# Attention scores of a hybrid trunk: keys stored once, two heads on the two row halves of the array

## The chip, the core and the metric

The kernel runs on one core of a Trainium2 chip. A core has TensorE (PE, the matrix unit; its weight loads are shown as PEld), VectorE (DVE), ScalarE (ACT), GpSimd (POOL) and SyncE (SP), which issues most of the DMAs. Each engine takes its own instructions in the order in which they stand, and waits on semaphores for the others. The metric is the device time of one execution in microseconds, lower is better; the figure compared is the median of several runs.

## The reference

A two-layer decoder trunk for 256 tokens with 1024 features, all in float32. Layer 0 mixes tokens by native sparse attention (NSA), layer 1 by RWKV-7; each is followed by a squared-ReLU MLP. The change touches NSA alone. It has 16 heads of width 64 in 4 groups; the 4 heads of a group share keys and values. Three branches are added with learned gates: compressed keys, selected blocks and a window. With 256 tokens all causal blocks are selected and the window covers everything, so these two branches see the same causal mask and differ in their keys and values:

```
s_s = einsum(q, k_selected) * scale ; p_s = softmax(where(valid_s, s_s, -1e30))
s_w = einsum(q, k_window)   * scale ; p_w = softmax(where(valid_w, s_w, -1e30))
o   = g0 * (p_c @ v_compressed) + g1 * (p_s @ v_selected) + g2 * (p_w @ v_window)
x   = x + concat(o) @ w_out
```

## The kernel before

Weights are streamed from HBM in 512 KB chunks and split into two float32r parts (ACT makes the high one on line 229, DVE the low one on line 231), and every product with weights is the sum of three matmuls (lines 265 to 267). The layer's work is written out once, as a list of steps in `NSA_ORDER`; a scheduler that simulates a timeline then fixes the order of the instructions of PE, ACT, DVE and POOL, and which of the free PSUM slots a tile gets. Only SP's queue stands as written. PSUM is one pool with two tags of four slots, each slot one 2 KB bank: `pmm` for tiles that PE fills and others read soon, `pacc` for accumulators.

The steps that matter here: `T0` and `T1` run `keys()` and `queries()`, which transpose keys and queries on PE. `qT[gp]` holds two heads of a pair one above the other: head s=0 in partitions 0 to 63, head s=1 in 64 to 127. The two heads belong to the two groups of a group pair. `kT[gp]` holds the keys of both groups, once for each s, with the other group's 64 partitions set to zero by a memset on POOL, so that a matmul over all 128 rows gives the scores of one head.

Steps `s0` to `s7` run `scores(pr)` for the eight pairs of heads. For a head, query tile t=0 sees 128 keys and t=1 sees 256, in both branches: one matmul 128x256 (S0, line 623) and one 128x512 (S1, line 625). The two S0 of a pair share one PSUM tile; each S1 has its own. On line 630 DVE adds the mask, takes the maximum, and writes the masked scores `e` to SBUF, once for a branch; ACT then makes the exponentials (line 634). `weigh` scales `e` (DVE, line 649), transposes it on PE (lines 652 to 654, tiles p) and copies the result out (lines 656, ACT and 659, DVE). `values` accumulates the output `po` of a pair: first the compressed branch, whose probabilities `pcT` come from `compressed(gp)` (transposes pcp on line 708, copy on DVE on line 709), as a matmul of 32 rows (line 665), then the two other branches with one head in each column half of the array (lines 670 and 673). Lines 674 and 675 take `po` out. Around these steps PE has the projection of the second half of the queries (acc), and after them the product with `w_out`, for which all `po` are wanted.

The RWKV layer is not touched by the change. Four of its names come up: for a chunk of tokens PE makes pZ (lines 1170, 1172), ACT copies it to Zt (line 1173), PE makes pQ from Zt (line 1179), and ACT copies pQ to VS (line 1180). ACT also squares the layer's output (ysq, line 1223), which belongs to the normalisation of an earlier chunk.

Of the kernel before, what the change touches and what calls it, by code (L numbers as in the profile page):

```python
# [9 lines left out]
F32 = mybir.dt.float32  # L10
# [23 lines left out]
# per-feature vectors, [128, 8] columns each  # L34
# [5 lines left out]
LAG = 2           # feed-forward tiles between the two products of the MLP  # L40
TAIL = 4          # weight chunks at the end of a product that are used by one token tile after the other
NF = DFF // 128
NPERM, NMID, NSLOT = 12, 18, 29       # 4 KB slots: for all layers, from the first feed-forward layer on, with RWKV's


def _mlp_order():
    """(product, feed-forward tile) in the order of use."""
    o, done = [], 0
    for f in range(NF):
        o.append((0, f))  # L50
        if f >= LAG and done < NF - TAIL:
            o.append((1, done))
            done += 1
    return o + [(1, f) for f in range(done, NF)]


# ---------------------------------------------------------------- host layout
def _consts():
    """Arrays that depend on shapes alone, side by side in one [128, n] block."""
# [20 lines left out]
    # cumulative sums about the middle of a chunk: columns t = -1 .. C-1  # L80
# [91 lines left out]
# ---------------------------------------------------------------- the kernel  # L172
@with_exitstack
def trunk(ctx: ExitStack, tc: tile.TileContext, wb, x_in, wg, cw1k, cw1v, cw2, vecs_in, l1, w2, a2, g2, rows,
# [44 lines left out]
    # ---- weights: streamed in 1 MB chunks, cut into two float32r parts  # L219
# [18 lines left out]
    # 4 KB slots, handed out in program order  # L238
# [24 lines left out]
    def mm3(o, lh, ll, rh, rl, first, last):  # L263
        """o += (lh + ll).T @ (rh + rl), without the product of the two low parts."""
# [20 lines left out]
    def after_split():  # L285
        """What this block traces on ACT and DVE comes after the last split of a layer's input."""
# [6 lines left out]
    def transposed_split(src, gv, h, l, t, name, cbs=(0, 1)):  # L293
        """h + l = (src * g).T, columns of token tile t."""
# [15 lines left out]
    def gemm_parts(hT, lT, evac, ncols, ahead=None):  # L310
        """Token-major product with the next weight chunks, 512 columns at a time."""
# [15 lines left out]
    def out_proj(hT, lT, name, after, tail=TAIL, hold=(), own=2):  # L327
        """x += (hT + lT).T @ the next weight chunks, then after(t): one token tile at a time, from the last chunks on."""
# [29 lines left out]
        for t in range(NT):  # L358
            # the second tile's first half of the columns ends before its second one
# [71 lines left out]
    # ================================================================ NSA  # L431
    def nsa():
        with ExitStack() as es:
            pool = es.enter_context(tc.tile_pool(name="nsa", bufs=1))
            kc = [big([128, 2 * G, 2, DH], f"kc{t}") for t in range(NT)]   # every head twice
# [897 lines left out]
```

## Time and profile before

| | us |
|---|---|
| runs shown | 761.9, 762.09, 764.71 (median 762.09) |
| span of the profiled execution | 758.7 |
| PE busy, share | 742.6, 98% |
| DVE busy, share | 468.5, 62% |
| ACT busy, share | 422.7, 56% |
| PE share of the chain that ended last | 96% |

The span reaches from the first to the last instruction of one profiled execution; the time of that execution itself is not given, and the span lies 3.4 us under the median of the runs. The scores, from the first S to the last `po`, stand between 69 and 140 us. A matmul in float32 is written as two records, its two passes through the array, and matmuls overlap in the records, so the time that one takes is better read from start to start than from its duration. "x2" in a row of the timeline counts records.

### The profile page before, as it was taken

The page shows a single profiled execution, that of the slowest core. Times are in us where ns is not written, and L with a number is a line of the kernel's source. Part 1 is how long each engine was busy: PE and PEld are TensorE (multiplying, and loading weights), DVE is VectorE, ACT ScalarE, POOL GpSimd, SP SyncE. Part 2 cuts the span into 40 slices and gives each one's busy share as a digit, 9 for nine tenths or more (in the row PEclk, how much of TensorE's full clock was granted, in tenths as well). Part 3 has the DMA queues.
Part 4 walks back from the last instruction along what each step waited for, and adds up shares of the span by engine and source line. Part 5 has one row for each costly group of instructions (what it writes and reads, how often), then busy time and mean ns, then how long its engine had stood idle before and what let it go on. Part 6 is the DMA issues. An engine that isn't in the chain of part 4 may idle for free.

```text
span 758.7 us, 13485 instructions
## 1 busy us (share of the span) xinstructions
PE 742.6 (98%) x5286; PEld 634.4 (84%) x5286; DVE 468.5 (62%) x963; ACT 422.7 (56%) x870; POOL 61.1 (8%) x77
## 2 busy tenths in 40 slices
PE   7999999999999999999999999999999999999996
PEld 5876866789989989888898885798989889989995
DVE  5767798358454455567856698546667444544553
ACT  6627587247555555563656642444729465565562
POOL 1000000000000000001012610136110000000000
PEclk9999999999999999999999999699999999999999
DMA  8956200218565555680152261320315655555531
GB/s 285 333 172 223 86 27 11 78 53 320 188 191 192 176 190 194 206 280 16 42 181 68 85 189 34 108 98 17 113 55 176 212 187 182 188 185 181 189 112 55
DMA packets 32013, 111.51 MB, mean 147 GB/s; under 512 B 3629, under 2 KB 4141, under 8 KB 31950
## 3 DMA queue, kind: packets, MB, share of 16 engines
q1 hardware_dynamic: 30590, 107.89, 42.7%
q10 hardware_dynamic: 1216, 2.24, 1.1%
q8 instruction: 41, 0.67, 0.4%
q0 software_dynamic: 144, 0.52, 0.2%
q14 instruction: 22, 0.18, 0.1%
HBM read 108.54 MB, written 1.05 MB: 144 GB/s over the span
## 4 chain that ended last, share of the span: by engine, by line
PE 96%; DVE 1%; issue 1%; DMA 1%; ACT 1%; SPq 0%; POOLq 0%; POOL 0%; ACTq 0%; DVEq 0%
PE mu L266 8%; PE mu L265 8%; PE mu L267 8%; PE mo L267 8%; PE mo L265 8%; PE mo L266 8%; PE acc L266 3%; PE acc L265 3%; PE acc L267 3%; PE pa L266 2%; PE pa L265 2%; PE pa L267 2%; PE S L625 2%; PE pM L1037 2%; PE po L670 1%; PE pL L975 1%
## 5 line engine op out<-in xcount | busy, mean ns | idle before, releaser
L231 DVE TENSOR_TENSOR wl<-wst,wh 128x1024 fp32r<-128x1024 f32 x175 | 214.3, 1229 | 177.2 <-ACT wh L229 176.4
L229 ACT ACTIVATE wh<-wst 128x1024 fp32r<-128x1024 f32 x175 | 184.4, 1058 | 166.7 <-PE mu L266 77.5
L266 PE MATMUL mo<-wl,mqh 128*128 128x512 f32 x224 | 88.4, 395 | 0.0
L265 PE MATMUL mo<-wh,mqh 128*128 128x512 f32 x224 | 88.2, 395 | 0.0
L267 PE MATMUL mo<-wh,mql 128*128 128x512 f32 x224 | 87.5, 397 | 0.0
L266 PE MATMUL mu<-m1l,wh 128*128 128x256 f32 x256 | 72.4, 284 | 0.0
L265 PE MATMUL mu<-m0h,wh 128*128 128x256 f32 x256 | 71.5, 281 | 0.4 <-DVE m0l L303 0.4
L267 PE MATMUL mu<-m1h,wl 128*128 128x256 f32 x256 | 71.8, 281 | 0.0
L265 PE MATMUL mu<-m1h,wh 128*128 128x256 f32 x256 | 71.6, 283 | 0.0
L266 PE MATMUL mu<-m0l,wh 128*128 128x256 f32 x256 | 71.6, 281 | 0.0
L267 PE MATMUL mu<-m0h,wl 128*128 128x256 f32 x256 | 71.5, 280 | 0.0
L267 PEld LDWEIGHTS mo<-wh,mql 128*128 128x128 f32 x224 | 42.1, 188 | 9.9
L266 PEld LDWEIGHTS mu<-m1l,wh 128*128 128x128 f32 x256 | 49.0, 191 | 1.1
L265 PEld LDWEIGHTS mu<-m0h,wh 128*128 128x128 f32 x256 | 48.1, 189 | 1.8 <-DVE m0l L303 0.6
L266 PEld LDWEIGHTS mu<-m0l,wh 128*128 128x128 f32 x256 | 48.3, 189 | 1.3 <-DVE m0l L303 0.2
L265 PEld LDWEIGHTS mu<-m1h,wh 128*128 128x128 f32 x256 | 48.2, 190 | 1.2
L266 PEld LDWEIGHTS mo<-wl,mqh 128*128 128x128 f32 x224 | 42.4, 189 | 8.2
L267 PEld LDWEIGHTS mu<-m1h,wl 128*128 128x128 f32 x256 | 49.1, 192 | 0.0
L265 PEld LDWEIGHTS mo<-wh,mqh 128*128 128x128 f32 x224 | 42.0, 188 | 7.8
L267 PEld LDWEIGHTS mu<-m0h,wl 128*128 128x128 f32 x256 | 48.3, 189 | 0.0
L265 PE MATMUL acc<-wh,n0h 128*128 128x512 f32 x80 | 31.8, 404 | 0.0
L267 PE MATMUL acc<-wh,n0l 128*128 128x512 f32 x80 | 31.4, 395 | 0.0
(365 smaller groups left out, 1577.9 us busy)
## 6 DMA issues: line engine op xcount, KB each, us to landing
wst<-in_wb_dram SPq DMA_DIRECT2D x188, 512.0 KB, 3.9
w1t<-in_cw1k_dram SPq DMA_DIRECT2D x4, 512.0 KB, 6.6
w1t<-in_cw1v_dram SPq DMA_DIRECT2D x4, 512.0 KB, 7.6
x<-in_x_dram SPq DMA_DIRECT2D x4, 256.0 KB, 5.0
rowt<-in_rows_dram ACTq DMA_DIRECT2D x2, 512.0 KB, 4.4
VS<-vt ACTq DMA_DIRECT2D x8, 128.0 KB, 2.4
out_dram<-xg SPq DMA_DIRECT2D x4, 256.0 KB, 2.1
g<-in_l_dram SPq DMA_DIRECT2D x2, 320.0 KB, 5.5
```

Source lines behind the costliest of these rows:

```text
L229: act(wh, st, AF.Copy)
L231: V.tensor_tensor(wl, st, wh.bitcast(F32), op=ALU.subtract)
L265: mm(o, lh, rh, start=first, stop=False)
L266: mm(o, lh, rl, start=False, stop=False)
L267: return mm(o, ll, rh, start=False, stop=last)
L625: mm(S1, qT[gp][:, hg, 128:256], kT[gp][:, s], start=True, stop=True)
L670: mm(po[s * 64:(s + 1) * 64, :S], vv[:, 0, vs], pt0[s][:, b], start=False, stop=False)
L975: mm(p[rows_of(k0), c, j], BK[k0 // 2][rs, j, c, k0 // 4], AR[k0 // 2][rs, j, c, 0], start=True, stop=True)
L1037: mm(p[:, j], BK[k // 2][rs, k % 2, c].rearrange("p a s -> p (a s)"), AR[k // 2][rs, k % 2, c].rearrange("p a s -> p (a s)"), start=True, ...
```

## The change

Keys are stored once: `kT[gp]` loses its group axis, the four memsets go, and one copy of 128 partitions takes the place of two copies of 64. Each score matmul uses 64 rows: partitions `s*64` to `s*64+63` of queries and keys, so that the two heads of a pair are two tiles on the two row halves of the array. The number of matmuls and their columns stay. Every matmul of a pair has its own PSUM tile (four instead of three), and the four are written in the order (s, t) = (0,0), (1,1), (0,1), (1,0). What reads the tiles stays.

```diff
-                    kT.append(big([128, 2, 2, S], f"kT{gp}"))
-                    for s in range(2):
-                        P.memset(kT[gp][(1 - s) * 64:(2 - s) * 64, s], 0.0)
+                    kT.append(big([128, 2, S], f"kT{gp}"))
...
-                    for s in range(2):
-                        V.tensor_copy(kT[gp][s * 64:(s + 1) * 64, s], p[s * 64:(s + 1) * 64])
+                    V.tensor_copy(kT[gp], p)
...
-                S0s = pmm([128, 2, 2, 128], "S0")
+                S0s = [pmm([128, 2, 128], "S0") for _ in range(2)]
+                S1s = [pmm([128, 2, S], "S1") for _ in range(2)]
+                for s, t in ((0, 0), (1, 1), (0, 1), (1, 0)):
+                    rs = slice(s * 64, (s + 1) * 64)
+                    if t:
+                        mm(S1s[s], qT[gp][rs, hg, 128:256], kT[gp][rs], start=True, stop=True)
+                    else:
+                        mm(S0s[s], qT[gp][rs, hg, 0:128], kT[gp][rs, :, :128], start=True, stop=True)
                 for s in range(2):
-                    S0 = S0s[:, s]
-                    mm(S0, qT[gp][:, hg, 0:128], kT[gp][:, s, :, :128], start=True, stop=True)
-                    S1 = pmm([128, 2, S], "S1")
-                    mm(S1, qT[gp][:, hg, 128:256], kT[gp][:, s], start=True, stop=True)
+                    S0, S1 = S0s[s], S1s[s]
```

The line numbers of what follows the scores shift by two: line 630 becomes 632, 649 becomes 651, 665 becomes 667, 709 becomes 711; S0 is now line 625 and S1 line 623. The scheduler gives PE, DVE and ACT another order. Three places follow; the numbers behind a name only tell tiles apart.

On PE, from the scores of pair 3 (before S_990, S_992, S_1005; after S_987 to S_990) to the first output `po`, with pair 4's scores between. Before:

```order
L623 MATMUL S_990<-kT_484,qT_660 128x256
L625 MATMUL S_992<-kT_484,qT_660 128x512
L625 MATMUL S_1005<-kT_484,qT_660 128x512
L623 MATMUL S_1021<-kT_494,qT_933 128x256
L708 MATMUL pcp<-cst,ce_930 128x128 x2
L623 MATMUL S_990<-kT_484,qT_660 128x256
L625 MATMUL S_1023<-kT_494,qT_933 128x512
L625 MATMUL S_1036<-kT_494,qT_933 128x512
L665 MATMUL po<-pcT,vcr 128x256
```

After:

```order
L625 MATMUL S_987<-kT_484,qT_654 128x256
L623 MATMUL S_990<-kT_484,qT_654 128x512
L623 MATMUL S_989<-kT_484,qT_654 128x512
L625 MATMUL S_988<-kT_484,qT_654 128x256
L625 MATMUL S_1019<-kT_491,qT_929 128x256
L710 MATMUL pcp<-cst,ce_926 128x128 x2
L623 MATMUL S_1022<-kT_491,qT_929 128x512
L623 MATMUL S_1021<-kT_491,qT_929 128x512
L625 MATMUL S_1020<-kT_491,qT_929 128x256
L625 MATMUL S_1148<-kT_491,qT_929 128x256
L667 MATMUL po<-pcT,vcr 128x256
```

Before, the S0 of the two heads share a tile, and other work stands between them. After, four scores of a pair or three of them stand next to each other, the remaining S0 apart, and one S0 of pair 5 (S_1148) moves ahead of the first `po`.

On DVE, the rows up to the copy of pcT for the first group pair, for which the first `po` waits. Before:

```order
L630 ISA e_1008,st<-S_1005,cst 128x256
L630 ISA st 128x1
L630 ISA e_1008,st<-S_1005,cst 128x256
L630 ISA st 128x1
L709 COPY pcT<-pcp 128x256
L649 TENSOR_SCALAR e_951<-e_951,st 128x128 x2
L649 TENSOR_SCALAR e_952<-e_952,st 128x256 x2
L649 TENSOR_SCALAR e_964<-e_964,st 128x128
```

After:

```order
L632 ISA e_1005,st<-S_988,cst 128x128
L632 ISA st 128x1
L632 ISA e_1005,st<-S_988,cst 128x128
L632 ISA st 128x1
L702 TENSOR_REDUCE cst_1121<-ce_983 128x16
L651 TENSOR_SCALAR e_951<-e_951,st 128x128 x2
L651 TENSOR_SCALAR e_952<-e_952,st 128x256
L632 ISA e_1027,st<-S_1019,cst 128x128
L632 ISA st 128x1
L632 ISA e_1027,st<-S_1019,cst 128x128
L632 ISA st 128x1
L651 TENSOR_SCALAR e_952<-e_952,st 128x256
L711 COPY pcT<-pcp 128x256
```

The copy, which stood right behind pair 3's reads of e_1008, now stands behind the last reads of pair 3 (e_1005), the reduction of the second compressed branch, four scalings of e and two reads of pair 4 (e_1027).

On ACT, in the RWKV layer, the copies Zt of one chunk and the squares ysq between them. Before:

```order
L1173 ACTIVATE Zt<-pZ 64x256
L1223 ACTIVATE ysq,gst<-y_5265 128x64 x3
L1173 ACTIVATE Zt<-pZ 64x256
L1223 ACTIVATE ysq,gst<-y_5265 128x64 x3
L1173 ACTIVATE Zt<-pZ 64x256
L1223 ACTIVATE ysq,gst<-y_5265 128x64 x2
L1173 ACTIVATE Zt<-pZ 64x256
L1180 ACTIVATE VS_4608<-pQ 64x4x64
L1223 ACTIVATE ysq,gst<-y_5265 128x64 x3
```

After:

```order
L1175 ACTIVATE Zt<-pZ 64x256
L1225 ACTIVATE ysq,gst<-y_5267 128x64 x8
L1175 ACTIVATE Zt<-pZ 64x256
L1225 ACTIVATE ysq,gst<-y_5267 128x64 x4
L1175 ACTIVATE Zt<-pZ 64x256
L1225 ACTIVATE ysq,gst<-y_5267 128x64 x4
L1175 ACTIVATE Zt<-pZ 64x256
L1182 ACTIVATE VS_4610<-pQ 64x4x64 x4
```

Eight squares in one go now stand between the first copy and the second, and four before each of the next two. Nothing in this layer's code has changed. The order on SP is as before, and POOL loses the four memsets.

## Rows read from the trace of the kernel before

**Rows 1.** The page: busy time, share and instructions of each engine.

```profile
PE 742.6 (98%) x5286; PEld 634.4 (84%) x5286; DVE 468.5 (62%) x963; ACT 422.7 (56%) x870; POOL 61.1 (8%) x77
```

**Rows 2.** Groups by line and shape, 69 to 130 us: count, busy us, mean ns, idle before.

```profile
L625 PE MATMUL S<-kT,qT 128*128 128x512 f32 x32 | 15.7, 599 | 0.0
...
L623 PE MATMUL S<-kT,qT 128*128 128x256 f32 x32 | 9.6, 388 | 0.3 <-ACT qT L610 0.3
```

**Rows 3.** Busy time of each engine in stretches of 10 us; PEclk is the granted clock.

```profile
core 0: us, PE busy (x) PEld busy (x) DVE busy (x) ACT busy (x) POOL busy (x), PEclk, DMA share, GB/s
70.00:80.00 10.00, 8.97 (x48) 6.09 (x48) 9.29 (x55) 8.30 (x35) 0.00 (x0) 1.00 0.08 32
...
100.00:110.00 10.00, 10.00 (x61) 5.96 (x60) 10.00 (x54) 8.67 (x30) 0.00 (x0) 1.00 0.00 0
```

**Rows 4.** Chain that ended last, 70 to 80 us: start us, us, what.

```profile
73.08 1.73 PE S L625 x4
...
74.83 0.42 DVE e L630
...
76.93 1.07 PE pv L583 x8
```

**Rows 5.** The same chain, from 95 to 101 us.

```profile
95.95 0.86 PE S L625 x2
...
100.74 0.43 PE S L623 x2
```

**Rows 6.** Timeline of PE: start us, us, what, records; 103 to 109 us.

```profile
103.47 0.69 PE L665 MATMUL po<-pcT,vcr 32*128 32x256 f32 x2
...
104.80 0.60 PE L670 MATMUL po<-pt,kw 128*64 128x256 f32 x4
105.23 0.39 PE L673 MATMUL po<-pt,kw 128*64 128x128 f32 x4
...
107.40 0.70 PE L623 MATMUL S<-kT,qT 128*128 128x256 f32 x2
108.03 0.44 PE L673 MATMUL po<-pt,kw 128*64 128x128 f32 x4
```

**Rows 7.** Timeline of PE, two row halves in the RWKV layer.

```profile
461.60 2.82 PE L1037 MATMUL pM<-AR,BK 64*128 64x128 f32 x32
464.35 1.12 PE L1057 MATMUL pg<-gw,gT 128*128 128x512 f32 x2
```

**Rows 8.** Timeline of DVE, 102 to 117 us; in brackets idle before it.

```profile
102.03 0.42 DVE L709 COPY pcT<-pcp 128x256 f32<-128x256 f32 x1
102.37 1.19 DVE L649 TENSOR_SCALAR e<-e,st 128x128 f32<-128x128 f32 x5
103.48 0.28 DVE L630 CUSTOM_DVE_ANT_0 e<-S,cst 128x128 f32<-128x128 f32 x1
...
104.32 0.80 DVE L649 TENSOR_SCALAR e<-e,st 128x128 f32<-128x128 f32 x3
105.04 0.41 DVE L700 TENSOR_REDUCE cst<-ce 128x16 f32<-128x256 f32 x1
...
116.72 0.42 DVE L630 CUSTOM_DVE_ANT_0 e<-S,cst 128x256 f32<-128x256 f32 x1 [1.40 <-PE p L654]
```

**Rows 9.** Busy PE and granted clock, 482 to 496 us.

```profile
482.00:496.00 14.00, 14.00 (x134) 0.51 0.24 76
```

**Rows 10.** Timeline of ACT, a chunk of the RWKV layer.

```profile
524.48 0.36 ACT L1173 ACTIVATE Zt<-pZ 64x256 f32<-64x256 f32 x1
524.75 0.24 ACT L1223 ACTIVATE ysq<-y 128x64 f32<-128x64 f32 x1
...
524.98 0.24 ACT L1223 ACTIVATE ysq<-y 128x64 f32<-128x64 f32 x1
...
526.60 0.38 ACT L1173 ACTIVATE Zt<-pZ 64x256 f32<-64x256 f32 x1
```

**Rows 11.** Timeline of PE, the same chunk.

```profile
527.03 0.68 PE L1179 MATMUL pQ<-Zt,TT 128*64 128x64 f32 x8 [0.34 <-ACT Zt L1173]
```

## The prediction

> **What bounds the kernel now.** I read the page first. PE is busy for 98% of the span, VectorE for 62% [rows 1], so whatever the change gives must come out of PE's path. The change touches the scores, so I looked next at that stretch alone, by line and shape. There are 32 records of each of the two score matmuls, two records a matmul, 16 matmuls of 128x512 and 16 of 128x256 [rows 2]. Their means, 599 and 388 ns, are pipelined durations and too long as a price. The chain, which counts from start to start, has 0.86 us for the two records of a 128x512 matmul and 0.43 us for a 128x256 [rows 5]. So a pair of heads costs 2 x 0.43 + 2 x 0.86 = 2.58 us of PE, and the eight pairs 20.6 us.
>
> Then the stretches of 10 us, since a share over the span says nothing of this stage. From 100 to 110 us PE is busy 10.00 of 10, but VectorE is too, 10.00; from 70 to 80 us PE has 8.97 and VectorE 9.29 [rows 3]. The stage has two full engines, and one of them gets no less work from this change: VectorE reads the same number of elements from the score tiles. The chain says who is late. From 69 to 74.8 us it goes over the eight scores of pairs 0 and 1, then over VectorE's reads and copies from 74.83 us, and comes back to PE with pv at 76.93 us [rows 4]. Behind that it stays on PE.
>
> **What it saves on PE.** An instruction keeps its columns, so by itself none gets shorter. The gain is two halves at work side by side. That halves do so in this kernel is in the trace: two 64-column tiles of 128x256, four records of 0.21 us each by the price above, stand 0.43 us apart from the next group [rows 6], half of 0.86. Row halves show it less fully: 32 records of pM with 128 columns, 0.107 us each, half of a 256-column record, would take 3.42 us one after the other and 1.71 us in pairs; the next matmul starts 2.75 us behind the first [rows 7].
>
> The order decides how much. PE takes its instructions in turn, and each half does one record at a time. Four in the written order then take 0.21 (first record of S0), then 0.43 + 0.43 for the S1 of the other half, with the two others following one record behind on each half: about 1.5 us instead of 2.58, a gain of 1.07. Three that are left when the first S0 is scheduled apart take 0.86 + 0.43 = 1.29 instead of 2.15, a gain of 0.86. A lone score gains nothing.
>
> Against this stands the switch between whole array and halves. A 128x256 score between two tiled `po` steps takes 0.63 us from start to start (107.40 to 108.03) where 0.43 is its work [rows 6]: 0.2 us for going in and out. After the change the scores are tiles and their neighbours (transposes, weights' products) are not. Going through the new order, behind pairs 0 and 1: pair 2 has one alone and three together (+0.2 - 0.86 + 0.2 = -0.46); pair 3 four and, behind them, one of pair 4 (-1.07 + 0.2); pair 4 three and one of pair 5 (-0.86 + 0.2); pair 5 then one alone and two together (+0.2 - 0.43 + 0.2); pair 6 two alone and two together (+0.17); pair 7 one and three (+0.1 - 0.66). Sum -2.4 us. Pairs 0 and 1, all eight together, would give -2 x 1.07 + 0.2 = -1.9.
>
> **What of it reaches the path.** Pairs 0 and 1: nothing. VectorE reads their tiles in one go, and PE's next work (pk, pv, then p) waits for copies on VectorE that stand in its queue among or behind these reads. The chain is on VectorE there [rows 4], and scores that are ready sooner wait in PSUM. I count 0 (between -0.3 and +0.3, since the order of the reads changes a little).
>
> Pairs 2 to 7: the copy of pcT is the place. Before, it starts at 102.03 us and is done some 0.4 us later, and the first `po` starts at 103.47, not held by it [rows 6, 8]. After, there stand ahead of it two reads of 128x128 (half of the four from 103.48 to 104.32, 0.42 us), a reduction (0.4), four scalings (four fifths of the five from 102.37 to 103.48, 0.9) and two more reads (0.42) [rows 8]: 2.1 us. VectorE has no idle time from which to pay this. So the copy starts at about 104.1, and the first `po` at about 104.9, 1.4 us later than before, though PE comes to it some 1.5 to 2 us earlier. From that 1.4 the score that stood between two `po` is to be taken (0.63, now ahead of the wait): PE is about 0.8 us behind at the end of these two outputs, having done 0.43 of S_1148 already, so 0.4 to 0.8. Nothing else fills the wait, since PE's queue holds it in order.
>
> From there on two things pull. PE has still some 0.6 us of the above sum to win (pairs 5 to 7: -0.03, +0.17, -0.56), and VectorE, once it runs short of work, catches up: it waits 1.40 us for PE at 116.72 [rows 8], and that slack takes up lateness. On the other side a pair now holds all four slots of the "mm" tag instead of three, so the next pair's scores can't be written ahead until VectorE has read. In the worst case one 128x512 score of each of the pairs 6 and 7 (0.86 each) waits with PE idle: +1.7. So the stage lies between -2.4 (nothing held up) and 0.9 + 1.7 = +2.6 us. I take 0, near the middle, because the wait on pcT is as large as the gain ahead of it.
>
> The Trainium skill, page "TensorEngine Tiling (Array Packing)", section "PSUM Bottleneck", says that tiling speeds up TensorE and not the emptying of PSUM, which may then be what limits. The trace agrees as far as VectorE's 10.00 of 10 us goes; taken alone the rule makes every gain here zero, and the sum would be the tail below.
>
> **The keys.** One copy of 128 partitions instead of two of 64, and four memsets on POOL less, all long before 69 us beside PE's weight products: 0 (-0.2 to 0, for what VectorE saves ahead of the first reads).
>
> **The RWKV layer.** Its order on ScalarE changes though its code does not. Before, the second of the four Zt starts at 524.48 and the last at 526.60; squares cost 0.24 us each from start to start (524.75 to 524.98) [rows 10]. After, 16 squares instead of 8 lie between the first Zt and the last: 8 x 0.24 = 1.9 more, less the 0.3 to 0.4 of waits between them before, so the last Zt comes 1.5 us later. pQ waits for it, as it did at 527.03 for 0.34 us [rows 11]. The copies VS behind it are now free of squares, which gives part back: counted through, the last products of the chunk are 0.9 us later. I take +1.0 (0 to +1.5).
>
> **Sum.** 758.7 + 0 + 0 + 1.0 = 759.7 us of span. The runs' median lies 3.4 us over the span, so 763.1 us.
>
> **The rivals.**
> - *The gain comes through.* VectorE gets its tiles earlier, works ahead, and the copy of pcT is not late; PE sets the stage. For it: the chain is on PE behind 77 us. Against it: 10.00 of 10 us on VectorE [rows 3]. -2.4 + 0 to 1: 760.7 (759.7 to 761.5); with pairs 0 and 1 too and no loss in the RWKV layer, 762.1 - 4.3 = 757.8. The Trainium skill, same page, section "Theoretical Speedup", gives up to twice the speed for a dimension of 64 or less; if every pair had it, that would be half of 20.6, 751.8, which the order and the full VectorE exclude.
> - *Slower: the slots run out.* The four tiles of a pair fill the four slots, PE stands before pairs 6 and 7 until VectorE has read, and the second pcT is late as the first. It decides if PE's waits on VectorE between 104 and 130 us exceed the 2 us won ahead. +2.6 + 1.5: 766.2 (765 to 767.5).
> - *The change doesn't do what it says.* The halves take their matmuls one after the other (pM went only half way [rows 7]). Then no gain, eight switches of 0.2, and the two losses: 762.1 + 1.6 + 0.9 + 1.0 = 765.6.
> - *The clock.* With half the rows and PE idle between 74 and 78 us, the granted clock falls to the lower level. In the stretch 482 to 496 us it was 0.51, in the RWKV layer with its small tiles, with PE busy all along [rows 9]; 14 us at half the clock are 7 us lost: 770. Against it: PE stood idle for over 1 us between 70 and 80 us already, and that stretch and the later one have 1.00 [rows 3].
>
> **How the numbers follow.** What a measurement can tell from no change is about 0.5%, 3.8 us: below 758.3 counts as faster, above 765.9 as slower. Forecast 0.50 (own range 761.5 to 765), gain 0.21, slots 0.20, no overlap 0.05, clock 0.04. Faster needs more than the full -2.4 of the gain: somewhat over half of its chance, allowing that my order walk is too strict, 0.12. Slower: 0.16 of the slots, 0.03, 0.04 and 0.02 from the forecast's edge, 0.25. The range, 758.4 to 767.0, leaves out the better end of the gain and the clock.
>
> **What would show it.** Right: groups of S in halves with starts a few ns apart; VectorE still near 10 of 10 from 100 to 115 us; the first `po` near 104.9, its idle time ended by the copy of pcT; the last Zt of that RWKV chunk some 1.5 us later against its first. Wrong: the first `po` before 103.5 and the last `po` of pair 7 more than 1.5 us earlier than before (the gain comes through); waits of S on VectorE over 1 us in pairs 5 to 7 (the slots); S starts 0.43 and 0.86 apart as before (no overlap); PEclk under 1.00 between 70 and 140 us.

## The result, and the profile after

The changed kernel takes 768.9 us (median of 4 runs, 767.49 to 771.26) against 762.37 for the kernel before: a ratio of 1.0091, 95% interval 1.0065 to 1.0117. It is slower, by more than the forecast of 763.1 and above the range of 758.4 to 767.0. Six further runs gave 769.1, ratio 1.0101 (1.0081 to 1.012). The ratios, here and below, are estimated from the fast runs alone and need not be the quotient of the medians, which count every run. The profiled execution has a span of 765.7 us against 758.7.

The page first: busy time, share and instructions of each engine, to be held against [rows 1].

```profile
PE 743.7 (97%) x5286; PEld 634.4 (83%) x5286; DVE 466.4 (61%) x961; ACT 422.5 (55%) x870; POOL 59.1 (8%) x73
```

PE is busy 1.1 us longer although its scores now share the array, and POOL and VectorE have the few instructions less that the diff removes. The page tells nothing more. What tells where the 7.0 us arose is the start of the same instruction in both traces, stage by stage:

| up to the start of | later than before by, us | added in the stage |
|---|---|---|
| first score S (70.68) | 0.86 | 0.86 |
| first p (79.68) | 1.83 | 0.97 |
| the 13th record of p (94.42) | 4.23 | 2.40 |
| first po (109.55) | 6.08 | 1.85 |
| 19th record of noa (wh, ol), the w_out product (159.22) | 6.34 | 0.26 |
| the 17th record of pT, RWKV (486.25) | 5.87 | -0.47 |
| first pY after it (506.79) | 5.15 | -0.72 |
| first roa (wl, yTh), product behind RWKV (551.63) | 6.91 | 1.76 |
| 141st record of mo (wh, mql), second MLP (625.81) | 6.99 | 0.08 |

The first 0.86 us is there already at the first products with weights and differs from trace to trace: the 11th record of acc (wh, n0h) starts at 16.65 us and 16.94 us in two traces of the kernel before, at 17.59 here, and in e2, e4 and e11, whose edits to the kernel before all lie behind it, at 17.80, 17.27 and 17.83. The rest has four places. "The end of NSA" below is the table's row of noa, and a dip is a stretch at the lower clock.

**Pairs 0 and 1.** The timeline of PE after the change (start us, us, engine, line, operation, records, in brackets the idle time before it and what ended it):

```profile
70.68 0.48 PE L625 MATMUL S<-kT,qT 64*128 64x256 f32 x1 [0.25 <-ACT qT L607]
70.69 0.69 PE L623 MATMUL S<-kT,qT 64*128 64x512 f32 x1
...
73.43 1.29 PE L623 MATMUL S<-kT,qT 64*128 64x512 f32 x3 [0.68 <-DVE st L632]
...
77.53 0.46 PE L573 MATMUL pk<-hids,w2t 128*64 128x64 f32 x8 [1.96 <-DVE hids L568]
77.92 1.97 PE L583 MATMUL pv<-w2t,hrep 128*128 128x64 f32 x8
79.68 0.42 PE L654 MATMUL p<-cst,e 128*128 128x128 f32 x1
79.89 0.42 PE L655 MATMUL p<-cst,e 128*128 128x128 f32 x1
```

The same place before the change:

```profile
76.07 0.46 PE L573 MATMUL pk<-hids,w2t 128*64 128x64 f32 x8 [0.62 <-DVE hids L568]
76.93 1.07 PE L583 MATMUL pv<-w2t,hrep 128*128 128x64 f32 x8 [0.41 <-DVE hrep L579]
77.85 0.28 PE L652 MATMUL p<-cst,e 128*128 128x128 f32 x1
```

Here pk and pv are PE's products for the compressed keys and values; they take hids, which VectorE copies out of PSUM, and hrep, a repeated copy of a part of it.

The first two rows show that the halves do work side by side: an S0 and an S1 of the other half start 7 ns apart. The first quartet takes 1.40 us to the next one's first record (72.08), where the prediction's prices give 2.58 for four scores with full rows. But the eight scores together end only about 1 us sooner against the first one than before, because PE stands still for 0.68 us ahead of what follows: the wait ends with VectorE's reads (st L632), as all four slots of the "mm" tag (`pmm`) are taken and VectorE has yet to read them. The wait before pk is 1.96 us where it was 0.62, so that PE idles for 2.64 us in this place, where it was 1.03 (0.62 and 0.41). VectorE's rows say why hids is later against the first score (6.4 us behind it, 5.8 before):

```profile
75.18 0.42 DVE L632 CUSTOM_DVE_ANT_0 e<-S,cst 128x256 f32<-128x256 f32 x1 [0.37 <-PE S L623]
...
77.06 0.42 DVE L568 COPY hids<-pht 128x256 f32<-128x256 f32 x1
```

VectorE itself waits 0.37 us for PE, the slots' wait coming back, and hids is queued behind all sixteen reads where it was ahead of the last two. The two rows of p above are 0.21 us apart; at the full clock it is 0.11 (e11 below shows both). The granted clock in stretches (behind the length stand PE's busy time with its count, the clock, the DMA share and GB/s) tells what happened:

```profile
76.00:78.00 2.00, 0.47 (x9) 0.98 0.03 8
78.00:80.00 2.00, 2.00 (x10) 0.50 0.00 0
...
84.00:86.00 2.00, 2.00 (x11) 0.82 0.00 0
```

From 77.9 to 84.7 us the clock is at its lower level of 1.2 GHz, 0.50; before it was 1.00 in the whole stage [rows 3]. PE had been idle for most of the two microseconds ahead of it (0.47 of 2.00 busy between 76 and 78 us). This is the 2.40 us of the table, and most of the 0.97 us of the row above it as well. pk starts 0.61 us later against the first score than before (6.85 us behind it, 6.24 before), and pv then finds hrep ready, which gives 0.48 back; but from pv to the first p pass 1.76 us at the lower clock where it was 0.92. Without that the first p would have come 0.1 us later, so the clock's share of the two rows is 3.2 us and that of the waits 0.1. In stretches of 10 us, with the columns of [rows 3]:

```profile
70.00:80.00 10.00, 7.11 (x40) 4.84 (x39) 9.01 (x54) 8.62 (x35) 0.00 (x0) 0.90 0.16 54
80.00:90.00 10.00, 10.00 (x41) 8.34 (x40) 4.64 (x18) 2.68 (x4) 0.00 (x0) 0.76 0.00 0
...
100.00:110.00 10.00, 8.03 (x42) 5.12 (x39) 9.48 (x55) 9.62 (x35) 0.00 (x0) 1.00 0.07 27
```

Between 70 and 80 us PE has 7.11 us of work instead of 8.97, although the last 2 us of it ran at the lower clock already: what the halves save has become idle time.

**The first po.** The timeline of PE from pcp to the first po:

```profile
105.31 0.53 PE L710 MATMUL pcp<-cst,ce 128*128 128x128 f32 x2 [0.51 <-DVE ce L707]
106.44 1.29 PE L623 MATMUL S<-kT,qT 64*128 64x512 f32 x3 [0.60 <-DVE st L632]
...
108.95 0.67 PE L625 MATMUL S<-kT,qT 64*128 64x256 f32 x2 [0.74 <-DVE st L632]
109.55 0.69 PE L667 MATMUL po<-pcT,vcr 32*128 32x256 f32 x2
```

And on VectorE's timeline the copy of pcT:

```profile
108.98 0.41 DVE L711 COPY pcT<-pcp 128x256 f32<-128x256 f32 x1
```

The first po starts 4.24 us behind pcp, where it was 2.46 (101.01 to 103.47). It has no idle time of its own: the copy that it needs is done at 109.39, and PE comes to it at 109.55, 0.60 us behind the start of the score ahead. It is this score (two records, the S_1148 that moved ahead of the first po) that waits 0.74 us, for its slot, until VectorE has made the two reads that stand one scaling ahead of the copy. Without this score the copy itself would have held po for nearly as long.

**The scores as a whole**, by line and shape, against [rows 2] (count | busy us, mean ns | idle before them and what ended it):

```profile
L623 PE MATMUL S<-kT,qT 64*128 64x512 f32 x32 | 13.3, 633 | 1.3 <-DVE st L632 1.3
...
L625 PE MATMUL S<-kT,qT 64*128 64x256 f32 x32 | 10.2, 410 | 1.0 <-DVE st L632 0.7 <-ACT qT L607 0.3
```

Before, the idle time in these groups was 0.3 us; now 2.0 us of PE's waits before a score end with a read of VectorE. The Trainium skill, page "TensorEngine Tiling (Array Packing)", section "Gotcha 1: PSUM Pressure", warns that row tiling raises the demand on PSUM, as different row tiles write to different banks. The trace agrees: these 2.0 us end with VectorE's reads of earlier scores, so they are waits for a slot, which is one bank.

**The RWKV chunk.** ScalarE's timeline, the first, second and last Zt, to be held against [rows 10]:

```profile
528.54 0.38 ACT L1175 ACTIVATE Zt<-pZ 64x256 f32<-64x256 f32 x1
...
530.74 0.37 ACT L1175 ACTIVATE Zt<-pZ 64x256 f32<-64x256 f32 x1
...
533.57 0.38 ACT L1175 ACTIVATE Zt<-pZ 64x256 f32<-64x256 f32 x1
```

And PE's last group of pQ, against [rows 11]:

```profile
534.00 0.68 PE L1181 MATMUL pQ<-Zt,TT 128*64 128x64 f32 x8 [0.81 <-ACT Zt L1175]
```

From the first to the last Zt pass 5.03 us, where it was 3.21 (523.39 to 526.60); PE waits 0.81 us instead of 0.34 in the last place and 0.68 once more ahead of it. The kernel's unchanged part has become 1.76 us longer. The order alone does this, without the halves or the four tiles: e4 and e11, made from the kernel before, have the same 16 squares between the first and the last Zt and lose 1.81 and 1.90 us in this row. Against that stands 1.2 us from a shorter stretch at the lower clock in RWKV, 487.5 to 501.2 us, where before it was 478.6 to 495.7; it is not the change's, as e8, the same kernel, has 17.1 us of it again.

### The profile page after: what moved, and what is told of

Its sections match the earlier page's. It is cut to its first block, busy times and chain, and to the rows that moved or that the text cites. A ratio compares the mean times of both kernels' runs of the same rounds, so it can differ in the third digit from the quotient of the medians.

```text
span 765.7 us, 13478 instructions
## 1 busy us (share of the span) xinstructions
PE 743.7 (97%) x5286; PEld 634.4 (83%) x5286; DVE 466.4 (61%) x961; ACT 422.5 (55%) x870; POOL 59.1 (8%) x73
## 4 chain that ended last, share of the span: by engine, by line
PE 93%; DVE 4%; ACT 1%; issue 1%; DMA 1%; SPq 0%; POOLq 0%; POOL 0%; DVEq 0%
PE mu L266 8%; PE mu L265 8%; PE mu L267 8%; PE mo L267 8%; PE mo L265 8%; PE mo L266 8%; PE acc L266 4%; PE acc L265 4%; PE acc L267 3%; PE pa L266 2%; PE pa L265 2%; PE pa L267 2%; PE pM L1039 2%; DVE e L632 1%; PE pL L977 1%; PE ph L546 1%
## 5 line engine op out<-in xcount | busy, mean ns | idle before, releaser
L266 PE MATMUL acc<-wl,n0h 128*128 128x512 f32 x80 | 32.5, 410 | 0.0
```

Of the source, the lines that this page charges most:

```text
L266: mm(o, lh, rl, start=False, stop=False)
```

## The experiments

All times are medians; ratios are against the kernel before on the same chip in the same job. Since the runs of one kernel differ by how long PE's clock was low in them, each trace is read by stages, and by the clock in them.

**e0. The kernel before once more.** No edit.

> The kernel before once more, for a second trace: 762.4 within 0.3%. It shows whether the 0.95 us by which the changed kernel's first products with weights start later (PE's acc at 17.59 instead of 16.65 us) comes with the change or from run to run, and whether the clock's dip in the RWKV layer (478 to 496 us) always has the same length. If the start belongs to the change, this trace has 16.65 again; if it varies from run to run, another value.

761.27 us, ratio 0.9992 (0.997 to 1.0013). Its acc starts at 16.94 us, and the stretch at the lower clock in RWKV is again some 17 us long. So the first products start 0.3 us later here without any edit, and up to 1.2 us later in e4, e2 and e11, whose edits lie behind them: the first 0.9 us of the table need no change. Of 27 runs of before in a later job 24 have a mean clock of 0.986 or 0.987, two of 0.983 (764.5 and 764.9 us), and one of 0.997 (755.5): 9 us between the ends of one program, and the clock differs with them.

**e1. The halves without the four tiles.**

```diff
-                S0s = [pmm([128, 2, 128], "S0") for _ in range(2)]
-                S1s = [pmm([128, 2, S], "S1") for _ in range(2)]
-                for s, t in ((0, 0), (1, 1), (0, 1), (1, 0)):
...
+                S0s = pmm([128, 2, 2, 128], "S0")
+                for s in range(2):
+                    rs = slice(s * 64, (s + 1) * 64)
+                    S0 = S0s[:, s]
+                    mm(S0, qT[gp][rs, hg, 0:128], kT[gp][rs, :, :128], start=True, stop=True)
+                    S1 = pmm([128, 2, S], "S1")
+                    mm(S1, qT[gp][rs, hg, 128:256], kT[gp][rs], start=True, stop=True)
```

> Half of the change alone: keys once and 64-row score matmuls, but the tiles and the writing order of before (one PSUM tile for both S0, so three tiles a pair). PE, VectorE and ScalarE then have nearly the order of before, the RWKV layer exactly. Theory A (the granted clock falls because PE, done sooner with the first eight scores, stands idle for VectorE's copy of hids; then the late pcT and the four tiles; then the RWKV order): pcT early again, RWKV loss gone, but the idle time before pk is longer than before's 0.62 us, over 1 us, and the clock may still fall for some 7 us, which costs 2.8: about 764, and 761 if it does not fall. Theory B (all of the loss comes from the order that the four tiles bring): no dip, 760 to 761.5. Theory C (64-row tiles in themselves lower the clock or run no faster): as slow as the changed kernel, 767 to 769, or S start to start as long as before.

766.08 us, ratio 1.0065 (1.0042 to 1.0089). In its trace the clock was 1.00 from 70 to 140 us, although PE waited 0.75 us ahead of the scores' second half, 0.45 before pk and 0.41 before pv, and the RWKV chunk was without the added 1.76 us (-0.1 against before). But the first po waited for pcT, as the timeline of PE shows:

```profile
102.14 0.44 PE L707 MATMUL pcp<-cst,ce 128*128 128x128 f32 x2
...
106.88 0.69 PE L664 MATMUL po<-pcT,vcr 32*128 32x256 f32 x2 [1.31 <-DVE pcT L708]
```

4.74 us behind pcp, with 1.31 us of idle time that ended with the copy of pcT: the scheduler had put the copy behind all eight scalings. My expectation that pcT would be early was wrong, and so the end of NSA is 2.1 us later from p's 13th record on, as in the changed kernel. So the late pcT needs no four tiles. The clock fell at another place, 399 to 402 us, in code that no edit touches and with PE busy all along (1.6 us); all nine runs have a mean clock of 0.984 or less.

**e2. The four tiles without the halves.**

```diff
-                S0s = pmm([128, 2, 2, 128], "S0")
+                S0s = [pmm([128, 2, 128], "S0") for _ in range(2)]
+                S1s = [pmm([128, 2, S], "S1") for _ in range(2)]
+                for s, t in ((0, 0), (1, 1), (0, 1), (1, 0)):
+                    if t:
+                        mm(S1s[s], qT[gp][:, hg, 128:256], kT[gp][:, s], start=True, stop=True)
+                    else:
+                        mm(S0s[s], qT[gp][:, hg, 0:128], kT[gp][:, s, :, :128], start=True, stop=True)
```

> The other half alone: 128-row score matmuls with zero rows as before, but four PSUM tiles a pair, written in the order (0,0), (1,1), (0,1), (1,0). PE has the same S work as before. Theory A: PE is busy with S until about 75.5 us, so no longer idle before pk than before and no dip there (PEclk 1.00 from 70 to 140 us); the copy of pcT is late as in the changed kernel and the first po waits some 1.5 us or more for it, pairs 6 and 7 wait for slots: 2 to 5 us over before by the end of NSA, RWKV as before: 764.5 to 767. Theory B: nearly the whole loss is here: 767 to 769. Theory C: none of it: 762 to 763.

765.12 us, ratio 1.0048 (1.0028 to 1.0068), as theory A had it. The work of S on PE is that of before, and yet the first p is 1.0 us later against the first S, and another 1.8 us are lost from p's 13th record to the end of NSA. So the four tiles and their order cost this much with full rows. The 1.0 us is not the changed kernel's 0.97, though. Here pk starts 7.7 us behind the first S, all at the full clock; in the changed kernel the halves have brought it back to 6.85, and the clock makes the rest (e1, halves with three tiles: 5.96; before: 6.24). And the second loss comes with either half of the change (e1: 2.1). In its trace the clock held behind this idle time of PE:

```profile
78.74 0.46 PE L573 MATMUL pk<-hids,w2t 128*64 128x64 f32 x8 [1.74 <-DVE hids L568]
```

**e3. The idle time filled.** The changed kernel with

```diff
+                for _ in range(9):
-                for j in range(2):
-                    nc.tensor.transpose(pht[:, j], y[:, j * 128:(j + 1) * 128], ident)
+                    for j in range(2):
+                        nc.tensor.transpose(pht[:, j], y[:, j * 128:(j + 1) * 128], ident)
```

> The changed kernel with the two transposes pht made nine times over (16 needless ones, some 1.7 us of PE in the time in which it waits for hids; the result is the same). The scheduler gives the RWKV layer the order of before as a side effect and moves pk and pv behind the first p. Theory A (the idle time lets the clock fall): PEclk 1.00 from 70 to 90 us, 2.8 us less there, and 1.8 us less in the RWKV chunk: 768.9 - 4.6 = about 764.3. Theory C (64-row tiles lower the clock): the dip stays, only the RWKV part goes: 767.

766.07 us, ratio 1.0059 (1.0038 to 1.008). Same columns as above, the clock where it had fallen:

```profile
76.00:78.00 2.00, 1.73 (x16) 1.00 0.03 8
78.00:80.00 2.00, 1.87 (x12) 1.00 0.00 0
```

1.00, and p's 13th record is 1.91 us later than before (1.14 of it from the later first score) instead of 4.23 (0.86 of it). The RWKV chunk is as before (-0.1). The median came out 1.8 us over the expected 764.3: five of the 12 runs lie at 763.4 to 764.6 us with a mean clock of 0.987 or more, and the other seven have 0.980 to 0.984; where it fell in these, no trace shows.

**e4. Idle time in the kernel before.** The copy hids twice, the first p held behind pv, and the step `H`, which makes hids, pk and pv, ahead of `w0`:

```diff
-NSA_ORDER = ("K a0 h0 h1 l2 q0 q1 q2 q3 h2 G l3 T0 s0 a1 h3 s1 w0 H q4 q5 q6 q7 w1 "
+NSA_ORDER = ("K a0 h0 h1 l2 q0 q1 q2 q3 h2 G l3 T0 s0 a1 h3 s1 H w0 q4 q5 q6 q7 w1 "
...
-                V.tensor_copy(hids.rearrange("p j a g n -> p j (a g n)"), pht)
+                for _ in range(2):
+                    V.tensor_copy(hids.rearrange("p j a g n -> p j (a g n)"), pht)
...
+                    with tc.issue_after(last_pv[0].ins) if pr == 0 else ExitStack():
```

> The kernel before, with 128-row scores, and only PE's wait before pk and pv made longer: the copy hids is done twice on VectorE, and the first transposes p are held behind pv, so that PE stands still between the eight scores and the first p for about 2.5 us instead of 1.0 (the result is the same). Theory A (idle time of PE at this place lets the clock fall, whatever the scores' rows): the mean clock of most runs falls below before's 0.986 to 0.987, and the trace, if it is one of these, has about 7 us at 0.5 behind 77 us; 761.5 + 1.7 + 3 = 766. Theory C (the 64-row tiles lower the clock): clock 0.986 to 0.987 in nearly all runs, 763.

766.42 us, ratio 1.0046 (1.0018 to 1.0074), but the profiled run is one of two of 12 at 757.6 and 758.0 us, with a mean clock of 0.998: no low stretch at all but at the very end. PE's waits there:

```profile
77.63 0.46 PE L576 MATMUL pk<-hids,w2t 128*64 128x64 f32 x8 [1.57 <-issue]
79.19 1.08 PE L586 MATMUL pv<-w2t,hrep 128*128 128x64 f32 x8 [1.10 <-DVE hrep L582]
80.10 0.28 PE L656 MATMUL p<-cst,e 128*128 128x128 f32 x1
```

1.57 and 1.10 us of idle time, and the clock stayed at 1.00, in this run. Nine of the other runs have 0.982 to 0.986. For the place behind 77 us this decides nothing; it is why e11 was made. Nor is PE's wait all that changed: ScalarE has the changed kernel's order in RWKV, which is 1.8 us of the time. The runs show the price of the clock, though: 10 us between runs of one kernel (757.6 at 0.998, 767.7 at 0.983).

**e5. The same code later.** The kernel before with

```diff
+                    if f == 0 and name == "0":
+                        for _ in range(20):
+                            mm(pu, w1h[:, 0], kt(h, 0), start=True, stop=True)
```

> The kernel before with 20 needless products of 128x256 at the start of the first layer's MLP, behind all of NSA: 20 x 0.115 = 2.3 us of PE, everything behind it 2.3 us later. In the traces of the two halves of the change the clock also fell for about 3.4 us at 398 to 402 us, in code that the change does not touch, and cost 1.6 us; in before's two traces it did not. Theory A1 (a later start of the same code is enough): mean clock 0.983 to 0.984 in many of the runs, 761.5 + 2.3 + 1.6 = 765.4. Theory A2 (that dip has another cause): 0.986 to 0.987 in nearly all runs, 763.8.

765.96 us, ratio 1.0045 (1.0029 to 1.0062). The trace has everything behind the addition 2.1 us later than e0's and nothing else: clocks as before, 761.3 us of span. But six of the 10 runs have a mean clock of 0.983 to 0.985, as only two of before's 27 have. So the shift costs its 2.1 us and, in most runs, 2 to 3 us of clock besides. That the low stretch lies at 398 us in those runs isn't shown: the profiled run is one of the others.

**e6 and e7. Another list of steps**, for the changed kernel and for the one before:

```diff
-             "C0 T1 s2 C1 s3 s4 P0 v0 v1 w2 P1 v2 s5 w3 s6 w4 v3 w5 v4 v5 w6 s7 v6 w7 v7").split()
+             "C0 P0 T1 C1 P1 s2 s3 v0 v1 w2 s4 v2 w3 s5 v3 w4 s6 v4 w5 s7 v5 w6 v6 w7 v7").split()
```

> The changed kernel with another list of steps: both compressed branches and their probabilities ahead of pairs 2 to 7 (C0 P0 T1 C1 P1 s2 s3 v0 v1 ...), so that VectorE copies pcT after 24 of the 64 score reads instead of 34. Theory A: the first po no longer waits for pcT, and the end of NSA comes 1.5 to 2 us earlier than in the changed kernel; RWKV in before's order, another 1.8; the clock's dip behind 77 us stays, as nothing is changed there: 768.9 - 3.5 = 765.4. If VectorE, full, sets NSA in any order: 767.

> The kernel before with the list of steps of the run above: the control for it. If the halves bring their gain once pcT is early, the end of NSA (the first product of the MLP) comes 1 to 2.5 us later here than in the run above, apart from the dip; if VectorE sets the pace, within 0.5 us. Time about 762 to 764.

767.73 us, ratio 1.0042 (1.0009 to 1.0075), and 766.95, ratio 1.0073 (1.0061 to 1.0085). Neither settles its question. In e7 the order put the second pcp ahead of the first po, and that pcp waited for VectorE: the first po is 4.67 us later than in the kernel before. In e6 the clock fell twice, from 77.8 to 84.6 us and again from 101.7 to 108.5. The first is one more trace of the fall behind the first eight scores; whether the halves gain with an early pcT, the two don't tell.

**e8. The changed kernel once more.** No edit.

> The changed kernel once more, for a second trace and more clocks: 768 to 769. Theory A: about 7 us at 0.5 behind 77 us in this trace too, and the mean clock of nearly all runs at 0.985 or lower, where before has 0.986 to 0.987 in 25 of 27. If the dip there was chance, this trace has 1.00 from 70 to 90 us and the time is 765 to 766.

769.1 us, ratio 1.0101 (1.0081 to 1.012). The dip is there again (77.2 to 84.0 us), and one more, as the clock (the third last number) in stretches shows:

```profile
78.00:80.00 2.00, 2.00 (x10) 0.50 0.00 0
80.00:84.00 4.00, 4.00 (x13) 0.50 0.00 0
...
402.00:404.00 2.00, 2.00 (x12) 0.50 0.53 207
```

All ten runs of the changed kernel have a mean clock of 0.985 or less, and nine of them 0.981 or less, as this trace; the one with 0.985 is the first profiled run, 767.49 us. In this trace the table's stages come out as 0.50, 1.23, 2.16, 1.85 and 0.23 us up to the end of NSA, then 1.6 for the dip at 401.5 to 404.9 us, and 1.75 for the RWKV chunk.

**e9. The changed kernel with pcT pinned.** VectorE may scale pair 2 only behind the copy:

```diff
+            pc_ins = [None, None]
...
+                    with tc.issue_after(pc_ins[0].ins) if pr == 2 else ExitStack():
...
-                V.tensor_copy(pcT[:, gp], p.rearrange("p t q -> p (t q)"))
+                pc_ins[gp] = V.tensor_copy(pcT[:, gp], p.rearrange("p t q -> p (t q)"))
```

> The changed kernel with one rule more for the scheduler: VectorE scales the e of pair 2 only behind the copy of pcT (of the first group pair), which so comes up in its queue ahead of all these scalings. As a side effect the RWKV layer has before's order. Theory A (first po waits for pcT behind other work of VectorE): the first po starts some 1 us earlier against pcp than in the changed kernel (there 4.2 us behind pcp), and the RWKV layer loses 1.8 us less: 766 with the dip behind 77 us, 763 without. If pcT is not what holds PE there, the first po moves by less than 0.3.

765.05 us, ratio 1.0034 (1.0015 to 1.0054). Its timeline of PE at pcp and the first po:

```profile
105.07 0.53 PE L713 MATMUL pcp<-cst,ce 128*128 128x128 f32 x2 [0.51 <-DVE ce L710]
...
108.66 0.69 PE L670 MATMUL po<-pcT,vcr 32*128 32x256 f32 x2
```

The first po is 3.59 us behind pcp instead of 4.24, less than the 1 us expected, but the wait of 0.74 us before the scores ahead of it has gone as well, and the order behind it is better: from p's 13th record to the end of NSA 0.73 us are lost where it was 2.11. The dip behind 77 us is there as expected, and the RWKV chunk is as before. 4 us of the loss go with one rule of order: 1.4 here, 1.85 in the RWKV chunk, and the trace has no dip at 400 us.

**e10. The halves in the order of before.** e1 with the rule of e9.

> Keys once and 64-row scores with the three tiles and the writing order of before, and the same rule on pcT: PE, VectorE and ScalarE have before's order but for a few neighbours. What is left is the 64-row tiles alone. Theory A (order and clock make the loss, the halves a small gain that VectorE hides): end of NSA within 1 us of before's apart from the start and any dip; 761 to 762 in runs with the clock at 0.986 or more. If 64-row scores cost time by themselves: 2 us or more behind before at the end of NSA at a clock of 1.00 there.

763.51 us, ratio 1.0026 (0.9996 to 1.0056): the only version that can't be told from the kernel before. Its trace has a short dip behind these waits of PE:

```profile
73.07 1.78 PE L624 MATMUL S<-kT,qT 64*128 64x512 f32 x4 [0.75 <-DVE st L629]
...
76.29 0.46 PE L573 MATMUL pk<-hids,w2t 128*64 128x64 f32 x8 [0.45 <-DVE hids L568]
77.16 1.84 PE L583 MATMUL pv<-w2t,hrep 128*128 128x64 f32 x8 [0.41 <-DVE hrep L579]
```

The clock, in the same columns:

```profile
76.00:78.00 2.00, 1.30 (x13) 0.81 0.00 0
78.00:80.00 2.00, 2.00 (x11) 0.50 0.04 8
80.00:82.00 2.00, 2.00 (x10) 0.83 0.00 0
```

Without the 1.7 us of that dip the end of NSA is 0.7 us later against the first S than before. Three of its runs have the mean clock of nearly all runs of before, 0.986 or 0.987, and take 761.2, 762.6 and 762.6 us; the kernel before took 761.7 in that job. So at this clock the halves by themselves bring nothing and cost nothing that the runs could tell; in the trace 0.3 us won up to pk stand against 1.0 lost from p's 13th record to the end of NSA. The clock is another matter. Six of the 12 runs have 0.982 or less, and the fall at 77.3 us came behind waits of 0.75, 0.45 and 0.41 us, shorter than those behind which the clock held with full rows (1.74 in e2, 1.57 and 1.10 in e4); in e1, with the same waits and the same halves, it held too. Whether half rows add to the cause stays open.

**e11. Longer idle time with full rows.** e4 with `range(3)`.

> The run e4 with the copy hids made three times: full 128-row scores, and PE still for over 3.5 us between the scores and the first p (e4: 1.57 + 1.10 us, its trace kept 1.00). Idle time alone as the cause: a dip of some 3 to 7 us behind 77 us in the trace, mean clock of nearly all runs at 0.985 or less, 766 to 768. Row halves as a needed part of the cause: 1.00 from 70 to 90 us, 764.5.

768.86 us, ratio 1.0097 (1.007 to 1.0124). The timeline of PE, idle time before pk, then two records of p 0.11 us apart and two later ones 0.21 us apart:

```profile
79.84 0.46 PE L576 MATMUL pk<-hids,w2t 128*64 128x64 f32 x8 [3.21 <-issue]
...
81.59 0.28 PE L656 MATMUL p<-cst,e 128*128 128x128 f32 x1
81.70 0.27 PE L657 MATMUL p<-cst,e 128*128 128x128 f32 x1
...
82.18 0.42 PE L657 MATMUL p<-cst,e 128*128 128x128 f32 x1
82.39 0.42 PE L658 MATMUL p<-cst,e 128*128 128x128 f32 x1
```

The clock in the stretch behind:

```profile
82.00:84.00 2.00, 2.00 (x11) 0.50 0.00 0
```

PE was idle for 3.21 and 0.38 us, and the clock fell at 81.9 us for about 3.4 us. All four runs have 0.985 or less. Idle time is enough; 64-row tiles are not needed for it. The time of this version holds more than that, 2.6 us of the longer waits, 1.7 of this dip and 1.9 in the RWKV chunk, whose order is the changed kernel's here too.

**e12. The idle time filled with half rows.** The changed kernel with

```diff
+                        for _ in range(5 if pr == 1 and s else 1):
-                        mm(S0s[s], qT[gp][rs, hg, 0:128], kT[gp][rs, :, :128], start=True, stop=True)
+                            mm(S0s[s], qT[gp][rs, hg, 0:128], kT[gp][rs, :, :128], start=True, stop=True)
```

> The changed kernel with its last 64-row score of pair 1 made five times over, 4 x 0.43 = 1.7 us of work on one row half in the time in which PE otherwise stands still for hids (the result is the same); as with the nine-fold pht, the scheduler moves pk and pv behind the first p. In that run the fill was 128-row transposes and the clock stayed at 1.00. Idle time as the cause: 1.00 from 70 to 90 us here too. Row halves as the cause (work on half the rows counts as little): the dip of about 7 us is there in spite of the fill.

765.7 us, ratio 1.0064 (1.0039 to 1.0089). PE and its clock in stretches:

```profile
76.00:78.00 2.00, 1.96 (x10) 1.00 0.05 8
78.00:80.00 2.00, 1.87 (x11) 1.00 0.00 0
...
106.00:110.00 4.00, 3.63 (x13) 0.50 0.00 0
```

With four needless scores on one row half in the idle time the clock stays at 1.00 here, as with transposes on all rows. So a stretch of half rows does not bring it down by itself, in the one trace there is. But it fell later, at 105.2 us, in the stretch in which PE waits for VectorE before the scores and the first po (0.51 and 0.60 us up to there).

## Why the prediction was wrong

*"Pairs 0 and 1: nothing."* This is the step that failed: counted at 0, within 0.3, it cost 3.4 us. That VectorE sets this place was right, and that scores which are ready sooner wait for it; at the full clock the first p would have come 0.1 us later, within the 0.3. I took from this that the time stays as it is. But a saving on an engine that waits for another one becomes idle time, 2.64 us instead of 1.03, and behind it the clock fell: 0.85 us from pv to the first p and 2.40 up to p's 13th record, 3.2 together. The fall is in all four traces of kernels with this order on PE (the changed one twice, e6, e9), gone with the idle time filled (e3, e12), and brought about with full rows by idle time alone (e11). How much idle time it takes is not shown (e10).

*The clock as a rival.* Its place and the idle time were named, "With half the rows and PE idle between 74 and 78 us"; the chance of 0.04 was far too small and the price of 7 us, taken from a stretch of 14 us [rows 9], too high. The fall lasted 6.8 us and cost 3.2. My reason against it, over 1 us of idle time already without a fall, is no reason: between 1.0 us without and 2.64 us with a fall nothing was known. Half the rows are not needed for it (e11); whether they help is open (e10).

*Pairs 2 to 7.* This term was mis-sized, 0 forecast and 2.1 measured. The lateness of the first po was forecast as 1.4 us; it is 1.85 in the table and in e8. The size was near, but the idle time is not ended by the copy of pcT, as I had it: it stands ahead of the score before po, which waits for a slot, and both hang on the same reads of VectorE. That the stage would win this back, and my middle of 0 between -2.4 and +2.6, failed. Little of the -2.4 came: PE's waits there add up to 2.6 us (0.51, 0.60 and 0.74 in the rows above, and 0.75 for a copy on ScalarE at 136.56 us), before it has none, and the stage is 2.1 us longer, so PE's own work got only some 0.5 us shorter, by this estimate. Most of the loss goes with the place of pcT and the order behind it: with pcT pinned 0.73 us are lost with four tiles (e9) and 0.98 with three (e10), with pcT late 2.1 with four and 2.1 with three (e1). I had both in the sum, and let a gain on PE stand against a wait for VectorE, which no gain on PE can shorten. The rival of the slots, +2.6, was nearest in size, but its place was wrong: no score of pairs 6 and 7 waits, those of pairs 1, 4 and 5 do.

*The RWKV layer.* +1.0 forecast, 1.76 measured. The last Zt came 1.8 us later against the first, where I had 1.5, and what I gave back for copies VS free of squares did not come, as PE waited twice. In e1, e2, e3, e9 and e10, whose ScalarE has the old order there, the chunk is within 0.1 us of before; in e4 and e11, which have the new one, it is 1.8 and 1.9 us longer.

*The keys and the overlap.* Right: nothing from the keys, and pairs of scores that start a few ns apart. The gain of 1.07 us for four together was well sized for the first quartet, which gained 1.18 against its price; over pairs 2 to 7 the sum of such gains was not.

Together: 0.9 from the start that is not the change's, 0.1 of waits in pairs 0 and 1, 3.2 of clock behind them, 2.1 of order and slots, 1.8 in RWKV and 0.1 behind it, less 1.2 of clock there, give the 7.0 us of span. What stays open is what half rows add to the fall of the clock, and where it fell in seven of e3's 12 runs and six of e5's 10; the traces show other runs.

## What to carry to other kernels

Before saving time on an engine, ask who waits for it: where another engine is full, the saving turns into idle time, and on PE idle time can cost the clock too. An edit to one step can move the order of everything that shares the pool and the scheduler, here by more than the change itself could give and as far off as another layer; compare orders first, and pin the copies for which the busiest engine waits. Compare runs at the same mean clock when an effect is below 1%.

## What had not been expected of the hardware

The lower clock makes runs of one program differ: 753.4 to 764.9 us for the kernel before in one job, at mean clocks of 0.997 to 0.983. It fell behind 2.64 us of idle time in two parts (0.68 and 1.96 us) in four traces of four, and in the traces at hand not behind 1.74 us (e2), nor behind 1.57 and 1.10 us in a run whose clock fell nowhere but at its very end (e4). Behind 0.75, 0.45 and 0.41 us it fell in one trace (e10) and held in another (e1). So the idle time in front of a place does not tell for certain whether the clock falls there. It fell without any idle time too: ahead of the 17 us at 0.50 in RWKV (before: 478.6 to 495.7 us) no wait of PE over 0.1 us stands in the 9 us before. And the same code, 2.1 us later in time, has the lower clock in more of its runs (e5: six of 10 at 0.983 to 0.985, before: two of 27 at 0.983).
